# One more SwiGLU pair by seven products, neighbouring tiles paired, and the last weights' sums moved

## The chip, the cores and the metric

The kernel runs on one core of one Trainium2 chip, in one launch. The metric is the device time of that launch in microseconds (us), the median of the runs; less is better. The engines are named as in the profile: PE is TensorE's matmul, PEld its weight load, DVE is VectorE, ACT is ScalarE, POOL is GpSimd, SP is SyncE, which here issues all DMAs (SPq is its queue).

## What is computed

One decoder block on 512 tokens of width 1024, everything in float32. The reference, cut to what matters:

```python
def reference(x, norm1_g, w_in, b_in, conv_..., lru_..., w_mix_out, norm2_g, ffn_w1, ffn_w3, ffn_w2, norm_f_g):
    h = rmsnorm(x, norm1_g)
    z = h @ w_in + b_in                                   # 512x1024 @ 1024x6656
    z_glu, z_rx, z_rg, z_ga, z_gb = split(z)
    u = z_glu[:, :1024] * sigmoid(z_glu[:, 1024:])
    u = silu(layernorm(causal_depthwise_conv(u, 31 taps)))
    y_a = u @ conv_w_out + conv_b_out                     # 1024x1024
    hb = rg_lru(causal_depthwise_conv(z_rx, 4 taps))      # gated linear recurrence
    y_b = (hb * gelu(z_rg)) @ lru_w_out                   # 1280x1024
    m = sigmoid(z_ga) * y_a + sigmoid(z_gb) * y_b
    x = x + m @ w_mix_out                                 # "mixing", 1024x1024
    h = rmsnorm(x, norm2_g)
    x = x + (silu(h @ ffn_w1) * (h @ ffn_w3)) @ ffn_w2    # 1024x2816 twice, 2816x1024
    return rmsnorm(x, norm_f_g)
```

## The kernel before

**Matmuls in three parts.** Every float32 operand is split into a high part (ScalarE casts it, L127) and a low part (VectorE or GpSimd subtracts, L123), and each product is made of three matmuls, high by high, high by low and low by high (`mm3`, L489). Activations lie as 128 channels by 512 tokens. A weight chunk is a 128 x 1024 tile of 512 KB: SP loads it into one of 4 `raw` buffers (L152, or L265, L334 and L337 for chunks of several loads), ScalarE casts it, and VectorE or GpSimd subtracts, into one of 5 `hl` buffers. Chunks are worked off in one written list; `weights(key)` asks for a chunk and has those up to 4 further on emitted too (`AHEAD`).

**Seven products instead of eight.** Some matrix products are made by a Winograd form of Strassen's scheme: both operands are cut into 2 x 2 quarters, seven products of quarters stand for eight, and sums of quarters are made beside. For the SwiGLU layer (the two products with `ffn_w1` and `ffn_w3`, 22 column tiles of 128, in 11 pairs) the pairs in `SEVEN` go that way: `ffn_seven(k)` makes seven products (L1131) of 24 matmuls each for each of the two matrices' halves, 168 in all with 256 columns, where a plain pair has 96 with 512. The sums of weight quarters (t1 to t4) of these pairs are made early by GpSimd in pieces (`make_f_sums`: two loads of 256 KB, L357; four subtractions or additions, L123 and L364; a store of the sums to DRAM, L368), a piece every few steps of the input products, and are loaded again as chunks when the pair's turn comes.

**Mixing and the last product** (`ffn_w2`) go through the class `Sevenfold` (matmuls at L938). A finished pair of tiles waits in `waiting` until `release` calls `pair`, which makes the operand's sums on VectorE: one 512-wide low part and five 256-wide steps. `run` then goes over the pairs twice: first three products a pair, then the others. The second loop's operands (`late`) are split by ScalarE and VectorE, two splits a pair. The weight sums of the last product are made in 22 pieces on VectorE during the SwiGLU pairs (`out_step`, numbers per pair in `OUT_PIECES`). `KEPT` says how many finished pairs stay waiting at which pair.

**The end of mixing** (`mix_end`) is an order written by hand for TensorE, ScalarE and VectorE: the last mixing products; six adds of their banks into the rows `x` (L888); mean squares and a root (L511, L512); scaling of the rows (L1020); transposes `th` (L529) that make the SwiGLU input from the first half of the rows, while TensorE does the rest; later the same for the second half (`xs`, then `th` again). GpSimd then adds the two parts of the transposed input (`hf`, L1105) for the quarter sums `hs`.

**Order elsewhere.** A list scheduler with its own costs orders each engine's instructions, and `issue_after` ties some of them behind a named instruction. Each engine and SP's queue run their instructions strictly in that order; a DMA that has to wait for a buffer or for data holds all DMAs behind it.

The functions that the change touches, with what calls them:

Of the kernel before, what the change touches and what calls it, by code (L numbers as in the profile page):

```python
# [8 lines left out]
F32 = mybir.dt.float32  # L9
# [81 lines left out]
def tile_block(ctx, tc, a, out):  # L91
# [154 lines left out]
    class Quartered:  # L246
        def __init__(self, name, w, kh, lo, parts=()):

            self.name, self.w, self.kh = name, w, kh
            self.parts = {n: [None] * kh for n in parts}  # L250
# [5 lines left out]
            def quarter(n, k):  # L256
                if n[0] == "t":
                    return self.sums[n, k]
                i, h = int(n[1]) - 1, int(n[2]) - 1
                return w[:, k + kh * i, h * T : (h + 1) * T]  # L260
# [19 lines left out]
        def order(self):  # L280
            return [j for k in range(self.kh) for j in (k, k + self.kh)]
# [17 lines left out]
        def make_sums(self, k):  # L299
            q = [raws.tile([P, 1024], F32, tag="raw", name=f"{self.name}ws{k}_{i}") for i in range(2)]  # L300
            for i, v in enumerate(q):
                nc.sync.dma_start(v, self.w[:, k + self.kh * i, :])
# [21 lines left out]
    f_sums = {k: dram.tile([P, 4, 1024], F32, tag=f"fs{k}", name=f"fs{k}") for k in SEVEN}  # L324

    def f_quarter(n, k, w_, c0, c1):

        c, j = 4 * (int(n[1]) - 1), k + KF * (int(n[2]) - 1)
        return w_[:, c + c0 : c + c1, j * P : (j + 1) * P]

    def f_chunk(n, k):
        def load(raw_t):
            if n[0] == "t":
                newest["any"] = nc.sync.dma_start(raw_t, f_sums[k][:, IN_PLACE.index(n), :]).ins  # L334
            else:
                for i, w_ in enumerate((w1, w3)):
                    newest["any"] = nc.sync.dma_start(raw_t[:, i * T : (i + 1) * T].rearrange("p (k n) -> p k n", k=4), f_quarter(n, k, w_, 0, 4)).ins  # L337

        wchunk(f"f{n}_{k}", load, 8, P, lo=vec)

    def f_piece(k, i, c):
        four = (w1, w3)[i].rearrange("p (h k) (e n) -> p h k e n", h=2, e=2)
        at = T * i + P * c
        halves = [four[:, h, c : c + 2, :, k * P : (k + 1) * P].rearrange("p k e n -> p e k n") for h in range(2)]
        return f"{k}_{i}_{c}", halves, f_sums[k][:, :, at : at + 256]

    def o_piece(k, c):
        four = outq.w.rearrange("p (h k) (e n) -> p h k e n", h=2, e=2)
        cs = slice(256 * c, 256 * c + 256)
        return f"o{k}_{c}", [four[:, h, k, :, cs] for h in range(2)], outq.all_sums[k][:, :, cs]  # L350

    def piece_load(name, halves):
        raw = wsums.tile([P, 1024], F32, tag="wsum", name=f"fws{name}")
        for h, src in enumerate(halves):
            to = raw[:, h * T : h * T + T]
            to = to.rearrange("p (e k n) -> p e k n", e=2, k=2) if len(src.shape) == 4 else to.rearrange("p (e n) -> p e n", e=2)
            nc.sync.dma_start(to, src)  # L357
        return raw

    def piece_sums(raw, eng):  # L360
        q11, q12, q21, q22 = (raw[:, 256 * m : 256 * m + 256] for m in range(4))
# [5 lines left out]
    def piece_store(raw, dest):  # L367
        nc.sync.dma_start(dest, raw.rearrange("p (m n) -> p m n", m=4))  # L368

    def make_f_sums():  # L370
# [9 lines left out]
        while todo or sums_due or stores_due:  # L380
# [4 lines left out]
            if todo and n >= next_at:  # L385
# [5 lines left out]
                def sums(raw=raw, dest=dest):  # L391
                    with tc.issue_after(newest["sub"]):
                        piece_sums(raw, pool_e)
# [11 lines left out]
    for k in range(KF):  # L405
        if k in SEVEN:
            for n in ("b11", "b21", "b22", "t2", "t1", "t3", "t4"):
                f_chunk(n, k)
        else:
            for j in (k, k + KF):  # L410
# [487 lines left out]
    class Sevenfold:  # L898
        def __init__(self, q):
# [3 lines left out]
        def tile(self, j, make):  # L903

            k, i = j % self.kh, j // self.kh
# [4 lines left out]
            if i:  # L910
                self.waiting.append((k, *self.uv[k]))
                self.release()
# [27 lines left out]
        def run(self, sums, begun, end):  # L940
# [7 lines left out]
            late = []  # L948
            r1, r2 = ([bank(f"{n}{r}{i}") for i in range(2)] for r in ("r1", "r2"))
            r5 = [bank2(f"{n}r5{i}") for i in range(2)]  # L950
            for k in range(kh):
# [10 lines left out]
                late.append((split(f"{n}eb{k}", e, vec), split(f"{n}vb{k}", va, vec)))  # L962
# [48 lines left out]

    def mix_end(second, plus, r1, r2, r7, third):
        sc = [[longt(f"xs{t}{h}") for h in range(2)] for t in range(NT)]
# [10 lines left out]
        with tc.manual_schedule(engines={ET.PE, ET.Activation, ET.DVE}):  # L1024
# [23 lines left out]
            for t in (2, 3):  # L1048
                scaled(t, 0)

# [3 lines left out]
    o7 = Sevenfold(outq)  # L1054
    out_todo = [o_piece(k, c) for k in range(OUT_EARLY, KF) for c in range(2)]
    out_at, out_quota = [None, None], dict(OUT_PIECES)

    def out_step(k):
# [5 lines left out]
        if out_at[0]:  # L1064
            with tc.issue_after(newest["now"]):
                piece_sums(out_at[0][0], vec)
# [16 lines left out]
    first_two = [0, KF]  # L1083
# [37 lines left out]

    def ffn_seven(k):
        u_, v_ = longt(f"ou{k}"), longt(f"ov{k}")

        def product(ps, x_, w_, again=False):

            h, l = weights(f"f{w_}_{k}")
            for i in range(2):
                for c, (xh, xl) in enumerate(f_in[x_]):
                    for m, (lw, rx_) in enumerate(((h, xh), (h, xl), (l, xh))):  # L1130
                        pe.matmul(  # L1131
                            ps[:, HALVES[i]], lw[:, 4 * i + c, :], rx_, start=not (again or i or c or m),
                            stop=bool(i and c == 3 and m == 2), skip_group_check=True,
                        )

# [36 lines left out]
    for k in range(1, KF):  # L1172
# [4 lines left out]
        for j in (k, k + KF):  # L1177
# [6 lines left out]
    assert not out_todo  # L1184
# [6 lines left out]
    def loads(k):  # L1191

        if k < 2:
            out_step(None)
        elif k < 10:
            assert out_at == [None, None]
            t, h = divmod(k - 2, 2)
            nc.sync.dma_start(x2[t][h], x2_kept[t][h][:, :])
        else:
# [86 lines left out]
```

## Time and profile before

| | us |
|---|---|
| median of 3 runs | 804.78 (804.7, 804.78, 807.82) |
| profiled execution, whole | 805.14 |
| its span | 803.2 |
| input products and what runs beside them | 11 to 328 |
| products of the two mixers | 328 to 419 |
| mixing, second norm | 419 to 476 |
| first tiles by plain products (pairs 0 and 1) | 459 to 507 |
| seven SwiGLU pairs by seven products | 507 to 648 |
| two plain pairs (9 and 10) | 648 to 691 |
| last product and last norm | 691 to 803 |

The profile is one execution on the chip. Its page gives busy time and instruction count of each engine, and the chain of work that ended last, followed back from the end. Queries of the trace give the waits of an engine, its instructions in order of time (start, duration, engine, line, operation, output and inputs, count, and in brackets the idle time before and what ended it), and busy time by stretches (the length, then for each engine its busy time and in brackets its instructions, then the granted clock, the DMA engines' busy share and GB/s). A busy engine that is not on the chain sets no time by itself.

### The profile page before, as it was taken

Reading aid. Unit: us, or ns where it says so; the run is one execution under the profiler, and the core shown is the slowest. Engines: PE = TensorE matmul, PEld = TensorE weight load, DVE = VectorE, ACT = ScalarE, POOL = GpSimd, SP = SyncE. Lnnn points to the kernel's source line nnn. Section 1 sums busy time; section 2 is a strip of 40 time slices with the busy share of each in tenths; the row PEclk is TensorE's granted clock in tenths of the full one; section 3 lists DMA queues with packets and bytes.
Section 4 is the critical chain, followed back from the end, with each engine's and each line's share of the span. In section 5 each row is a group of like instructions: output and inputs, shape, how many; then the busy total and the mean of one; then the engine's idle time right before and its main releaser. Section 6 shows DMA issues by size and latency. Waiting matters only on the chain.

```text
span 803.2 us, 12106 instructions
## 1 busy us (share of the span) xinstructions
PE 792.8 (99%) x4254; PEld 687.7 (86%) x4254; DVE 676.3 (84%) x1080; ACT 457.8 (57%) x650; POOL 252.3 (31%) x203
## 2 busy tenths in 40 slices
PE   8999999999999999999999999999999999999996
PEld 7988888888888888888888898999999988888885
DVE  5799999998999998886798869979977796898556
ACT  7446788766589655653336454446555543476443
POOL 2576678756677684231320043000000000000000
PEclk9999999999999999999999999999999999999999
DMA  7746575666657743679988427699887979698552
GB/s 221 189 122 179 155 206 166 188 189 200 188 170 233 213 144 102 196 230 277 291 278 259 152 92 233 193 305 290 290 263 237 266 243 300 196 316 288 176 166 104
DMA packets 213871, 170.79 MB, mean 213 GB/s; under 512 B 13383, under 2 KB 188915, under 8 KB 213811
## 3 DMA queue, kind: packets, MB, share of 16 engines
q1 hardware_dynamic: 213811, 170.03, 69.6%
q8 instruction: 33, 0.54, 0.3%
q14 instruction: 27, 0.22, 0.1%
HBM read 134.47 MB, written 32.51 MB: 208 GB/s over the span
## 4 chain that ended last, share of the span: by engine, by line
PE 98%; DVE 1%; DMA 1%; ACT 0%; issue 0%; SPq 0%
PE z L489 35%; PE fr L1131 18%; PE or L938 13%; PE f L489 11%; PE yb L489 7%; PE ya L489 5%; PE mxr L938 5%; PE g L810 3%; DMA x<-in_x_dram 1%; PE z L582 0%; PE th L529 0%; PE tx L540 0%; DVE of L1209 0%; DVE x2b L888 0%; ACT n1j L511 0%
## 5 line engine op out<-in xcount | busy, mean ns | idle before, releaser
L683 DVE SCALAR_TENSOR_TENSOR cv<-u,par,cv 128x511 f32<-128x511 f32 (+17 forms) x240 | 162.6, 728 | 1.1 <-ACT cv L680 0.9
L123 POOL TENSOR_TENSOR hl_in<-raw_in,hl_in 128x1024 fp32r<-128x1024 f32 x51 | 123.1, 2417 | 82.6 <-ACT hl_in L127 61.1
L123 POOL TENSOR_TENSOR fws<-fws 128x256 f32<-128x256 f32 x84 | 70.8, 844 | 79.7 <-DMA fws<-in_ffn_w_dram 65.3
L127 ACT CAST hl_in<-raw_in 128x1024 fp32r<-128x1024 f32 x51 | 53.0, 1042 | 1.2 <-issue 1.0
L127 ACT CAST hl_ob<-raw_ob 128x1024 fp32r<-128x1024 f32 (+1 forms) x23 | 23.4, 1016 | 37.1 <-PE f L489 16.1
L1131 PE MATMUL fr<-hs_0h,hl_ft 128*128 128x256 f32 x224 | 41.5, 283 | 0.0
L489 PE MATMUL z<-h10h,hl_in 128*128 128x512 f32 (+1 forms) x110 | 41.4, 378 | 0.0
L123 DVE TENSOR_TENSOR hl_ft<-raw_ft,hl_ft 128x1024 fp32r<-128x1024 f32 x28 | 34.0, 1219 | 8.7 <-ACT hl_ft L127 8.7
L489 PE MATMUL z<-h11h,hl_in 128*128 128x512 f32 (+1 forms) x110 | 41.1, 376 | 0.0
L489 PE MATMUL z<-h17h,hl_in 128*128 128x512 f32 (+1 forms) x110 | 41.1, 376 | 0.0
L489 PE MATMUL z<-h13h,hl_in 128*128 128x512 f32 (+1 forms) x110 | 41.1, 376 | 0.0
L489 PE MATMUL z<-h14h,hl_in 128*128 128x512 f32 (+1 forms) x110 | 41.1, 376 | 0.0
L489 PE MATMUL z<-h15h,hl_in 128*128 128x512 f32 (+1 forms) x110 | 41.1, 376 | 0.0
L489 PE MATMUL z<-h16h,hl_in 128*128 128x512 f32 (+1 forms) x110 | 41.1, 376 | 0.0
L489 PE MATMUL z<-h12h,hl_in 128*128 128x512 f32 (+1 forms) x110 | 41.1, 376 | 0.0
L123 DVE TENSOR_TENSOR hl_ob<-raw_ob,hl_ob 128x1024 fp32r<-128x1024 f32 (+1 forms) x23 | 27.1, 1177 | 15.8 <-ACT hl_ob L127 15.5
L127 ACT CAST hl_ft<-raw_ft 128x1024 fp32r<-128x1024 f32 x28 | 29.3, 1048 | 15.4 <-issue 5.2
L123 DVE TENSOR_TENSOR hl_fb<-raw_fb,hl_fb 128x1024 fp32r<-128x1024 f32 x21 | 26.7, 1273 | 13.1 <-ACT hl_fb L127 13.1
L1131 PEld LDWEIGHTS fr<-hs_0h,hl_ft 128*128 128x128 f32 x224 | 35.4, 192 | 0.0
L127 ACT CAST hl_fb<-raw_fb 128x1024 fp32r<-128x1024 f32 x21 | 22.0, 1049 | 22.9 <-DMA raw_fb<-in_ffn_w_dram 9.7
L1131 PE MATMUL fr<-hs_0l,hl_ft 128*128 128x256 f32 x112 | 31.7, 283 | 0.0
L123 DVE TENSOR_TENSOR hl_ot<-raw_ot,hl_ot 128x1024 fp32r<-128x1024 f32 (+1 forms) x17 | 20.0, 1191 | 11.5 <-ACT hl_ot L127 11.2
(938 smaller groups left out, 2608.0 us busy)
## 6 DMA issues: line engine op xcount, KB each, us to landing
raw_in<-in_w_in_dram SPq DMA_DIRECT2D x52, 512.0 KB
fws<-in_ffn_w_dram SPq DMA_DIRECT2D x56, 256.0 KB
fs<-fws SPq DMA_DIRECT2D x28, 512.0 KB
raw_ft<-fs SPq DMA_DIRECT2D x28, 512.0 KB
fwso<-in_ffn_w_dram SPq DMA_DIRECT2D x44, 256.0 KB
ot<-fwso SPq DMA_DIRECT2D x22, 512.0 KB
raw_fb<-in_ffn_w_dram SPq DMA_DIRECT2D x42, 256.0 KB
raw_ob<-in_ffn_w_dram SPq DMA_DIRECT2D x33, 256.0 KB
```

The lines of the kernel that those rows point to most:

```text
L123: return eng.tensor_tensor(out=o, in0=x, in1=y, op=ALU.subtract)
L127: copy(h, full)
L489: pe.matmul(ps, l, r, start=i == 0, stop=i == n - 1)
L683: vec.scalar_tensor_tensor(out=acc[c][:, s:], in0=u[c][:, : T - s], scalar=dw(c, s), in1=acc[c][:, s:], op0=ALU.mult, op1=ALU.add)
L810: pe.matmul(ps, l, r, start=k == 0, stop=k == len(mms) - 1)
L938: pe.matmul(banks[i], l_[:, ts], r_, start=start and n == 0, stop=stop and n == 2, skip_group_check=again)
L1131: pe.matmul(ps[:, HALVES[i]], lw[:, 4 * i + c, :], rx_, start=not (again or i or c or m), stop=bool(i and c == 3 and m == 2), skip_group_c ...
```

## The change

- Pair 9 of the SwiGLU layer goes by seven products too: eight pairs do, three are plain (0, 1 and 10).
- Pair k is made of the neighbouring tiles 2k and 2k + 1 instead of k and k + 11. The second quarter row of weights is loaded for both tiles in one chunk (256 columns in a run), one chunk for each of `ffn_w1` and `ffn_w3`, and so are the sums; a chunk then serves two products, and the first product's chunk stays as it was.
- The 16 further instructions of sums on GpSimd come with a denser plan (from step 34 on every second step, before from step 55).
- Three of the 22 pieces of the last weights' sums are made by GpSimd inside `mix_end`; the other 19 stay on VectorE, spread differently.
- More finished pairs stay waiting (`KEPT`, up to 6), and the last stage's first loop releases one of them per step. Its late splits start at its sixth step instead of its first.

```diff
-OUT_PIECES = {1: 4, 2: 2, 3: 1, 4: 2, 5: 1, 6: 1, 7: 1, 8: 2, 9: 4, 10: 4}
-SEVEN = (2, 3, 4, 5, 6, 7, 8)
+OUT_PIECES = {1: 4, 2: 2, 3: 1, 4: 2, 5: 2, 6: 1, 7: 2, 8: 1, 9: 2, 10: 2}
+SEVEN = (2, 3, 4, 5, 6, 7, 8, 9)
-SUMS_DENSE = 55
-KEPT = {5: 1, 6: 2, 7: 3, 8: 4, 9: 2}
+SUMS_DENSE = 34
+OUT_MIX, LATE_LAG = 3, 5
+KEPT = {4: 1, 5: 2, 6: 3, 7: 4, 8: 5, 9: 6, 10: 6}
...
-        wchunk(f"f{n}_{k}", load, 8, P, lo=vec)
+        wchunk(f"fb11_{k}", load, 8, P, lo=vec)
+        for n in ("b2", "t0", "t1"):
+            for i, w_ in enumerate((w1, w3)):
+                if n == "b2":
+                    src = w_[:, 4:8, 2 * k * P : 2 * (k + 1) * P]
+                else:
+                    src = f_sums[k][:, i, int(n[1]), :].rearrange("p (k n) -> p k n", k=4)
+                wchunk(f"f{n}{i}_{k}", src, 4, 2 * P, lo=vec)
...
-outq = Quartered("o", a["ffn_w2"][0].rearrange("(k p) n -> p k n", p=P), NF // 2, vec)
+outq = Quartered("o", a["ffn_w2"][0].rearrange("(k p) n -> p k n", p=P), NF // 2, vec, step=2)
...
 # Sevenfold.run, first loop
-                late.append((split(f"{n}eb{k}", e, vec), split(f"{n}vb{k}", va, vec)))
+                if k >= self.lag:
+                    split_late()
                 begun(k)
 # second loop
                 second(k, *get(k, "b22", "t2", "t3"))
+                split_late()
...
     def mix_end(second, plus, r1, r2, r7, third):
+        made = []
+        for _ in range(OUT_MIX):
+            name, halves, dest = out_todo.pop(0)
+            with tc.issue_after(newest["any"]):
+                made.append((piece_load(name, halves), dest))
+            piece_sums(*made[-1], pool_e)
...
+        for m in made:
+            with tc.issue_after(newest["any"]):
+                piece_store(*m)
...
-    o7 = Sevenfold(outq)
+    o7 = Sevenfold(outq, LATE_LAG)
...
 # ffn_seven: product
-            h, l = weights(f"f{w_}_{k}")
+            n, e, first = WHERE[w_]
             for i in range(2):
+                if n == "b11":
+                    if i == 0:
+                        got["b11"] = weights(f"fb11_{k}")
+                    h, l = (v[:, 4 * i : 4 * i + 4, :] for v in got["b11"])
+                else:
+                    if first:
+                        got[n, i] = weights(f"f{n}{i}_{k}", AHEAD - i)
+                    h, l = (v[:, :, e * P : (e + 1) * P] for v in got[n, i])
...
+                if i == 0 and n != "b11" and not first:
+                    emit_to(emitted[0] + 1)
...
 # last stage's first loop
     def loads(k):
-        if k < 2:
-            out_step(None)
+        o7.release(max(len(o7.waiting) - 1, 0))
+        out_step(("or", k))
```

More of the change, by code (lines that the diff above doesn't have):

```diff
@@ L280, in order @@
         def order(self):
-            return [j for k in range(self.kh) for j in (k, k + self.kh)]
+            return [self.tile(k, i) for k in range(self.kh) for i in range(2)]
         def get(self, k, *names, ahead=AHEAD):
@@ L898, in tile_block, with __init__ @@
     class Sevenfold:
-        def __init__(self, q):
+        def __init__(self, q, lag=0):
+            self.lag, self.kept = lag, 0
             self.q, self.uv, self.ops, self.waiting = q, [], [], []
@@ L911, in tile @@
                 self.waiting.append((k, *self.uv[k]))
-                self.release()
+                self.release(self.kept)
         def release(self, keep=0):
@@ L948, in run, with split_late @@
             late = []
+            def split_late():
+                k = len(late)
+                if k < kh:
+                    late.append((split(f"{n}eb{k}", self.ops[k][2], vec), split(f"{n}vb{k}", self.ops[k][3], vec)))
             r1, r2 = ([bank(f"{n}{r}{i}") for i in range(2)] for r in ("r1", "r2"))
@@ L1010, in tile_block @@
     xs = []
+    out_todo = [o_piece(k, c) for k in range(OUT_EARLY, KF) for c in range(2)]
     def mix_end(second, plus, r1, r2, r7, third):
+        made = []
[4 more added lines that the diff above has]
+            piece_sums(*made[-1], pool_e)
         sc = [[longt(f"xs{t}{h}") for h in range(2)] for t in range(NT)]
@@ L1176, in tile_block @@
         o7.release(KEPT.get(k, 0))
-        for j in (k, k + KF):
+        o7.kept = KEPT.get(k, 0)
+        for j in (2 * k, 2 * k + 1):
             p1, p3 = bank(f"f1_{j}"), bank(f"f3_{j}")
```

72 lines of the change are left out of this document (37 added, 35 removed).

## The prediction

> **What bounds the kernel now.** I read the page first (engine shares, the chain that ended last), then the waits of the matmul engine, then windows by stage, then the timelines of VectorE, ScalarE, GpSimd and the DMA queue around mixing.
>
> ```profile
> span 803.2 us, 12106 instructions
> PE 792.8 (99%) x4254; PEld 687.7 (86%) x4254; DVE 676.3 (84%) x1080; ACT 457.8 (57%) x650; POOL 252.3 (31%) x203
> PE 98%; DVE 1%; DMA 1%; ACT 0%; issue 0%; SPq 0%
> ```
>
> The third line is the chain's share by engine. TensorE works 792.8 of 803.2 us; what is left is the start, 7 us of tail and about a microsecond of waits. Nothing shortens this kernel by more than the matmul time it removes plus those ends. The chain in order of time prices the two ways of doing a SwiGLU pair (columns: start, us, what):
>
> ```profile
> 506.57 141.11 PE fr L1131 x1176
> 647.68 43.55 PE f L489 x192
> ```
>
> L1131 holds the seven-product matmuls (256 columns), L489 here the plain ones (512 columns). Seven pairs are 1176 = 7 x 168 matmuls: 141.11 / 7 = 20.16 us a pair, 0.120 us each. Two plain pairs are 192: 43.55 / 2 = 21.78 us a pair, 0.227 us each. Windows over one seven-product pair, the last plain pair and the first part of the last stage (columns: length, then busy us of PE, PEld, DVE, ACT, POOL, then clock, DMA share, GB/s):
>
> ```profile
> 546.90:567.10 20.20, 20.20 (x170) 20.20 (x170) 18.91 (x32) 12.70 (x20) 0.00 (x0) 1.00 0.95 300
> 627.60:647.70 20.10, 20.10 (x169) 20.10 (x168) 14.32 (x21) 10.37 (x14) 0.00 (x0) 1.00 0.93 277
> 669.50:691.20 21.70, 21.70 (x97) 17.96 (x96) 12.45 (x27) 6.01 (x8) 0.00 (x0) 1.00 0.78 251
> 691.20:725.00 33.80, 33.80 (x151) 27.99 (x150) 32.51 (x55) 23.19 (x33) 0.00 (x0) 1.00 0.85 275
> ```
>
> TensorE is full in each at clock 1.00; VectorE is full only where the last stage begins.
>
> **Part 1, one more pair by seven products (pair 9).** It removes 96 plain matmuls and adds 168 short ones: 20.16 - 21.78 = -1.62 us, all on the path. On VectorE it adds three weight splits of 1.22 us and five adds of 0.68 us, 7.1 us, in a pair where it was busy 21.17 of 21.8 us already (from 647.7). Much of that was sums of waiting pairs, which part 4 moves; what remains is a normal seven-product pair, 14.32 us in 20.1. Cost nothing; if that cover failed it would be a few us.
>
> The Trainium skill ("TensorE: Matmul & The Clock Gate", Back-to-back issue gap) gives N/2.4 + 2.5 ns for an isolated matmul: by estimate 109 ns at 256 columns and 216 ns at 512, so 18.3 against 20.7 us, a saving of 2.4 us instead of 1.62 and 803.2 us in the end. The trace differs: 0.120 and 0.227 us, with the weight loads busy for all of each seven-product window, and its rows decide.
>
> **Part 2, neighbouring tiles paired, weights of two tiles loaded together.** Pair k is now tiles 2k and 2k+1. Two thirds of the unsummed seven-product weights come in runs of 256 columns instead of 128, with the same bytes. The DMA share was 0.87 to 0.98 in the first four such pairs and no matmul waited, so this can only help what already costs nothing. The price is a buffer held over two products: of five split buffers, the shortest lead is from the middle of a pair's third product to the middle of its sixth, three products of 24 x 0.120 = 2.88 us: 8.64 us instead of the former four, 11.5. Cast (1.05) and split (1.22) with the longest waits in these pairs (4.2 for a load, 2.3 for the cast) make 8.8 in the worst case, which rarely falls together. Taken at nothing, at most 0.2 us a pair, 1.6 in all.
>
> **Part 3, GpSimd's share.** First, four more pieces of summed weights for pair 9, taken more densely from step 34 on. That is 16 instructions at 0.844 us, 13.5 us, beside the input products. Between 205 and 305 us GpSimd is busy some 73 of 100 us. Its low-part splits (2.4 us) could now queue behind one or two pieces (3.1 us each), against four chunks of 5.44 us in hand: nothing. The last piece is loaded about one product step (5.44 us) later, so the DMA queue's wait for its sums, which ended at 412.3, ends near 418; the mixing weight behind it is needed by TensorE at 435: nothing.
>
> Second, three pieces of the last weights' sums run on GpSimd in the end of mixing: 12 instructions at 0.74 to 0.84 us, 9 to 10 us. GpSimd stood idle there for 60 us, but its neighbour does not. Timeline rows of VectorE (start, us, ..., idle before in brackets), the last two of them beside GpSimd's L1105 adds:
>
> ```profile
> 447.41 1.22 DVE L123 TENSOR_TENSOR hl_f<-raw_f,hl_f 128x1024 fp32r<-128x1024 f32 x1 [1.43 <-ACT hl_f L127]
> 448.56 4.07 DVE L888 TENSOR_TENSOR x<-mxr,x 128x512 f32<-128x512 f32 x6
> 453.72 0.89 DVE L1020 TENSOR_SCALAR xs<-x,stats 128x512 f32<-128x512 f32 x2
> 476.90 4.03 DVE L123 TENSOR_TENSOR hl_f<-raw_f,hl_f 128x1024 fp32r<-128x1024 f32 x2
> 486.77 2.31 DVE L123 TENSOR_TENSOR hl_fb<-raw_fb,hl_fb 128x1024 fp32r<-128x1024 f32 x1
> ```
>
> A 1024-wide split takes 1.22 us alone and 2.0 (4.03 / 2) to 2.31 us beside GpSimd. The split at 447.41 runs straight into the six adds, these into two squares and roots, these into the scaling at 453.72, and TensorE begins the transposes that read the scaled rows at 454.45, with about 0.2 us to spare. The three loads are queued behind one weight load that was issued at 438.96; six issues of 0.63 us and some 3 to 4 us to land put GpSimd's sums at about 444 to 455. So this split grows by 4.03/2 - 1.22 = 0.8 us; the 0.2 to spare set against one stretched scaling, TensorE waits 0.8. Bounds: nothing, if the sums fall elsewhere or the slack holds; 1.7 us if three of the scalings (0.44 us each) are stretched in the same ratio, 0.29 each. Adds that read PSUM beside GpSimd kept their time (0.74 at 407.38), so I take 0.8, the row nearest in kind.
>
> The Trainium skill ("GPSIMD Engine Reference", Specifications) says that GpSimd shares its SBUF interfaces with VectorE and that contention arises with instructions that have two SBUF inputs or run in a two-port mode. The splits agree (2.0 against 1.22); no row here shows a scaling beside GpSimd, and by the page it would be stretched too, which by estimate would make the wait 1.7 us rather than 0.8.
>
> The stores of these sums stand on SP's queue ahead of the loads of pair 1's weights, which were issued from 440 to 450 before and now go at about 456. ScalarE casts the first of them near 462; landing near 460 it is in time. This is a rival below.
>
> **Part 4, sums of waiting pairs beside the last stage.** A pair's sums are a 512-wide split and five 256-wide steps; by the distance of their starts in the timeline, 0.60 + 5 x 0.335 = 2.3 us. Before, one pair's (the last) fell in the last stage; now six are released there, one per step, though the changed order starts several before the stage begins, in the 21.70 - 12.45 = 9.3 us that VectorE idles in the last plain pair. That is up to 5 x 2.3 = 11.4 us more at the stage's start; against it 5 x 2 late splits (0.60 each, 6.0 us) go to the second half of the stage, and two fewer pieces of weight sums (8 x 0.335 = 2.7 us) reach it. Net 2.7 us, and the idle time ahead of the stage covers it: nothing. Without that cover it is 2.7 us at most.
>
> **Sum.** -1.62 + 0.8 = -0.8 us. The profiled execution took 805.14 (span 803.2 and 1.94 around it), 0.36 over the median of 804.78. So 804.3 on its scale, **804.0 us** on that of the median.
>
> **Rivals.**
>
> - *Clean gain*: the mixing sums miss the split. For it: loads may land late. Against: the transposes start on the heels of the scaling. 804.78 - 1.62 = 803.2.
> - *Slower, through SP's queue*: the piece at 347.56 shows GpSimd taking 4.49 us for two instructions, 2.25 each, beside VectorE. Twelve at that rate take 27 us, to 471. The store then holds SP until then, pair 1's weights land at 475, and ScalarE's in-order queue has their cast ahead of the squares for the second half of the rows, whose transposes were due at 470.5. Cast, square, root, scale (some 4 us) follow: transposes at 479, 8.5 us late: 804.8 - 1.6 + 8.5 = 811.7. It decides once the twelve average over about 1.55 us (sums to 463, weights at 467.5, rows at 471). Against: 0.74 to 0.84 in nearly all pieces, and VectorE's work there mostly reads PSUM.
> - *VectorE becomes the bound where the last stage begins*: released sums stand ahead of weight splits on its queue, TensorE waits for weights. Full price 2.7 us on top of the forecast: 806.7. Against: pairs are ready four to five steps of 4.08 us ahead.
> - *Weight lead too short in the seven-product pairs*: 8 x 0.2 = 1.6 us, 805.6.
> - *The change doesn't do what it says*: more is saved because some wait goes that I don't see. TensorE's waits sum to 3.2 us, 2.7 of them at the start, which stays; so hardly below 801.
>
> **How the numbers follow.** About 0.5% (4 us) is what a measurement of this kernel can tell from no change. Chances: forecast 0.60, clean gain 0.17, short lead 0.07, VectorE 0.06, SP's queue 0.08, unseen gain 0.02. The likeliest is 804.0 with its own range 803.1 (no wait) to 804.9 (1.7 us wait). The range takes in the clean gain less 0.6 for run-to-run spread, 802.6, and the short lead and nearly the whole VectorE case, 806.6; SP's queue stays out. Faster by over 0.5% (below 800.8): 0.02. Slower (above 808.8): SP's queue, 0.08. Same: 0.90.
>
> **What would show it.** In the changed profile: 4326 matmuls; 1344 at the seven-product line in 161.3 us; GpSimd rows on the last weights at about 444 to 455; the split ahead of the six adds at 2.0 us instead of 1.22; a gap of 0.5 to 1 us on TensorE ahead of the first transposes and no other new one. A gap ahead of the second transposes, or at the first products of the last stage, would make the prediction wrong; so would a seven-product pair over 20.3 us.

## The result, and the profile after

The changed kernel took 804.29 us (median of 22 runs, 803.82 to 805.72) against 805.5 us for the kernel before in the same runs (22 runs, 804.67 to 807.97). The medians lie 1.21 us apart. The ratio is 0.9982, 95% interval 0.9976 to 0.9988 (it leaves disturbed runs out), which on 805.5 us is 1.45 us less, 1.0 to 1.9. The forecast was 804.0 us and 0.8 us less. The profiled execution took 804.0 us with a span of 802.2, 1.0 us under the span before.

From the page of the changed kernel, its size, the work of each engine and the shares of the chain of waits:

```profile
span 802.2 us, 12279 instructions
PE 791.7 (99%) x4326; PEld 690.6 (86%) x4326; DVE 680.1 (85%) x1076; ACT 463.0 (58%) x658; POOL 273.9 (34%) x231
PE 96%; DVE 1%; DMA 1%; ACT 0%; issue 0%; SPq 0%; DVEq 0%
```

There are the 72 more matmuls (168 - 96), and 28 more instructions on GpSimd (16 and 12). The third line is the chain: TensorE's share fell from 98% to 96%. The chain in order of time (start, us, what) shows where it left TensorE. Before:

```profile
419.09 35.36 PE mxr L938 x156
454.45 0.87 PE th L529 x8
```

After:

```profile
418.72 27.21 PE mxr L951 x120
...
448.97 1.90 DVE x L900 x3
...
452.36 1.64 DVE xs L1049 x2
...
454.10 0.77 DVE xs L1049
454.92 0.98 PE th L541 x7
...
507.13 161.27 PE fr L1177 x1344
668.40 21.79 PE f L501 x96
690.19 102.97 PE or L951 x453
```

(L951 was L938, L541 was L529, L1049 was L1020, L1177 was L1131, L501 was L489, L900 was L888, L126 was L123.) Before, the mixing products ran unbroken for 35.36 us into the transposes. Now the chain leaves TensorE for the adds and scalings of VectorE, and the transposes (all but the first) wait for the third scaling. TensorE's waits (us in total, times, longest) have it as the only one that was not there before:

```profile
PE th L541 <- DVE xs L1049: 0.7, 1, 0.7
```

Further down the chain stand eight seven-product pairs in 161.27 us and one plain pair in 21.79.

The two spans compared piece by piece (starts of the chain's rows, us):

| from - to | before | after | difference |
|---|---|---|---|
| start to mixing | 419.09 | 418.72 | -0.37 |
| mixing to the first seven-product pair | 87.48 | 88.41 | +0.93 |
| pairs 2 to 10 | 184.66 | 183.06 | -1.60 |
| last stage and end | 111.97 | 112.01 | +0.04 |
| span | 803.2 | 802.2 | -1.00 |

The first row is chance (the kernel before, profiled once more below). So the profiles place -1.60 + 0.93 + 0.04 = -0.63 us; the interval of the ratio begins at -1.0. The 0.4 us or more between them has no place in any trace here.

VectorE and GpSimd where the transposes wait (timeline rows: start, us, engine, line, operation, what, in brackets the idle time ahead):

```profile
447.04 1.22 DVE L126 TENSOR_TENSOR hl_f<-raw_f,hl_f 128x1024 fp32r<-128x1024 f32 x1 [1.43 <-ACT hl_f L130]
...
452.36 1.64 DVE L1049 TENSOR_SCALAR xs<-x,stats 128x512 f32<-128x512 f32 x2
...
454.10 1.62 DVE L1049 TENSOR_SCALAR xs<-x,stats 128x512 f32<-128x512 f32 x2
```

```profile
447.05 1.81 POOL L377 TENSOR_TENSOR fwso<-fwso 128x256 f32<-128x256 f32 x1
...
451.28 0.74 POOL L377 TENSOR_TENSOR fwso<-fwso 128x256 f32<-128x256 f32 x1
452.10 2.48 POOL L126 TENSOR_TENSOR fwso<-fwso 128x256 f32<-128x256 f32 x3
```

The split began 0.01 us ahead of a GpSimd instruction. It kept its 1.22 us, and the GpSimd instruction took 1.81 instead of 0.74. The scalings came into a row of GpSimd instructions, and two of them took 1.64 us instead of 0.89. In both meetings the one that began first kept its time. The Trainium skill ("SBUF — State Buffer", Who interferes with whom) calls this an exclusive lock on a pair of ports that the two engines share; of VectorE's two-port modes it says that whoever issues first holds the pair for the whole instruction while the other waits. These rows agree, and the split, which has two inputs, behaves the same way; a run below with 32 more instructions on GpSimd does not agree.

### The profile page after: what moved, and what is told of

The parts are those of the page before. It is cut to its first block, busy times and chain, and to the rows that moved or that the text cites. A ratio compares the mean times of both kernels' runs of the same rounds, so it can differ in the third digit from the quotient of the medians.

```text
span 802.2 us, 12279 instructions
## 1 busy us (share of the span) xinstructions
PE 791.7 (99%) x4326; PEld 690.6 (86%) x4326; DVE 680.1 (85%) x1076; ACT 463.0 (58%) x658; POOL 273.9 (34%) x231
## 4 chain that ended last, share of the span: by engine, by line
PE 96%; DVE 1%; DMA 1%; ACT 0%; issue 0%; SPq 0%; DVEq 0%
PE z L501 35%; PE fr L1177 20%; PE or L951 13%; PE f L501 8%; PE yb L501 7%; PE ya L501 5%; PE mxr L951 4%; PE g L822 3%; DMA x<-in_x_dram 1%; DVE x L900 0%; PE th L541 0%; PE z L594 0%; PE tx L552 0%; DVE xs L1049 0%; DVE of L1257 0%
## 5 line engine op out<-in xcount | busy, mean ns | idle before, releaser
L126 POOL TENSOR_TENSOR hl_in<-raw_in,hl_in 128x1024 fp32r<-128x1024 f32 x51 | 123.2, 2419 | 68.8 <-ACT hl_in L130 55.7
L126 POOL TENSOR_TENSOR fws<-fws 128x256 f32<-128x256 f32 x96 | 79.0, 825 | 83.7 <-DMA fws<-in_ffn_w_dram 79.4
L1177 PE MATMUL fr<-hs_0h,hl_ft 128*128 128x256 f32 x256 | 47.4, 283 | 0.0
L126 DVE TENSOR_TENSOR hl_fb<-raw_fb,hl_fb 128x1024 fp32r<-128x1024 f32 x24 | 30.4, 1267 | 18.8 <-ACT hl_fb L130 18.8
L126 DVE TENSOR_TENSOR hl_ft<-raw_ft,hl_ft 128x1024 fp32r<-128x1024 f32 x32 | 38.9, 1219 | 7.3 <-ACT hl_ft L130 7.3
L501 PE MATMUL z<-h10h,hl_in 128*128 128x512 f32 (+1 forms) x110 | 41.4, 378 | 0.0
L501 PE MATMUL z<-h17h,hl_in 128*128 128x512 f32 (+1 forms) x110 | 41.1, 376 | 0.0
L501 PE MATMUL z<-h11h,hl_in 128*128 128x512 f32 (+1 forms) x110 | 41.1, 376 | 0.0
L501 PE MATMUL z<-h16h,hl_in 128*128 128x512 f32 (+1 forms) x110 | 41.1, 376 | 0.0
L501 PE MATMUL z<-h14h,hl_in 128*128 128x512 f32 (+1 forms) x110 | 41.1, 376 | 0.0
L501 PE MATMUL z<-h13h,hl_in 128*128 128x512 f32 (+1 forms) x110 | 41.1, 376 | 0.0
L501 PE MATMUL z<-h15h,hl_in 128*128 128x512 f32 (+1 forms) x110 | 41.1, 376 | 0.0
L501 PE MATMUL z<-h12h,hl_in 128*128 128x512 f32 (+1 forms) x110 | 41.1, 375 | 0.0
L1177 PEld LDWEIGHTS fr<-hs_0h,hl_ft 128*128 128x128 f32 x256 | 40.5, 192 | 0.0
L130 ACT CAST hl_ft<-raw_ft 128x1024 fp32r<-128x1024 f32 x32 | 33.2, 1044 | 9.1 <-DMA raw_ft<-fs 2.9
L130 ACT CAST hl_fb<-raw_fb 128x1024 fp32r<-128x1024 f32 x24 | 25.2, 1050 | 21.3 <-DMA raw_fb<-in_ffn_w_dram 11.4
L1177 PE MATMUL fr<-hs_0l,hl_ft 128*128 128x256 f32 x128 | 36.2, 283 | 0.0
L126 DVE TENSOR_TENSOR hl_ob<-raw_ob,hl_ob 128x1024 fp32r<-128x1024 f32 (+1 forms) x23 | 26.9, 1175 | 10.5 <-ACT hl_ob L130 10.5
L1185 ACT ACTIVATE c<-c 128x256 f32<-128x256 f32 x24 | 10.1, 419 | 32.4 <-DVE c L900 32.4
```

What stands on the lines that cost most here:

```text
L126: return eng.tensor_tensor(out=o, in0=x, in1=y, op=ALU.subtract)
L130: copy(h, full)
L501: pe.matmul(ps, l, r, start=i == 0, stop=i == n - 1)
L1177: pe.matmul(ps[:, HALVES[i]], lw[:, c, :], rx_, start=not (again or i or c or m), stop=bool(i and c == 3 and m == 2), skip_group_check=True,)
L1185: act.activation(c[:, LO], c[:, LO], AF.Silu)
```

## The experiments

"Ratio" is always against the kernel before; unless said, an edit is made in the changed kernel.

**The last weights' sums back on VectorE.**

```diff
-OUT_MIX, LATE_LAG = 3, 5
-OUT_PIECES = {1: 4, 2: 2, 3: 1, 4: 2, 5: 2, 6: 1, 7: 2, 8: 1, 9: 2, 10: 2}
+OUT_MIX, LATE_LAG = 0, 5
+OUT_PIECES = {1: 4, 2: 2, 3: 2, 4: 2, 5: 2, 6: 2, 7: 2, 8: 2, 9: 2, 10: 2}
```

> The changed kernel with all 22 pieces of the last weights' sums on VectorE, none on GpSimd at the end of mixing. Theory (GpSimd's instructions hold up the scaling of the rows, and this is the only cost of the change): the 0.72 us gap ahead of the first transposes is gone, the two scalings take 0.89 us a pair again instead of 1.64, and the time is 0.7 us under the changed kernel, ratio to before about 0.9973 instead of 0.9982. Rival (VectorE has no room for three more pieces, 12 instructions of 0.42 us): the gap goes, but a new one of up to 5 us comes in the SwiGLU pairs or at the start of the last stage.

Measured: 804.09 us, ratio 0.9981 [0.9972, 0.999]. From its VectorE timeline:

```profile
452.00 0.89 DVE L1049 TENSOR_SCALAR xs<-x,stats 128x512 f32<-128x512 f32 x2
452.99 0.88 DVE L1049 TENSOR_SCALAR xs<-x,stats 128x512 f32<-128x512 f32 x2
```

Without GpSimd beside them the scalings take 0.89 us again, the wait at the transposes is gone, and mixing to the first seven-product pair is 87.46 us, as before the change (87.48). So the 0.93 us of that row come from the three pieces on GpSimd. VectorE made them during the pairs without a new wait: 183.16 us from pair 2 to the last stage (after: 183.06). The ratio does not resolve the 0.95 us between the two kernels; the profiled span, 801.6, is 0.6 us shorter. Chance is of that size here: mixing began 0.36 us earlier in this profile, and what follows the start of the last stage took 0.61 us longer (112.62 against 112.01).

**The order of the scalings changed**: the halves that the first transposes read are scaled first for both row tiles, the other two behind.

```diff
-            for t in range(2):
-                scaled(t, 1)
+            r_0 = rstd_end(begun[0], x2[0][1], sc[0][1])
+            scale(0, 0, r_0)
+            r_1 = rstd_end(begun[1], x2[1][1], sc[1][1])
+            scale(1, 0, r_1)
+            scale(0, 1, r_0)
+            scale(1, 1, r_1)
```

> The changed kernel with the four scalings in another order: the halves that the first transposes read go first. If a GpSimd instruction in flight holds a scaling off until it ends (a lock): two scalings instead of three stand before the first transposes, each waits for at most one GpSimd instruction (0.74 us), gap 0.2 us or none. If the two engines share bandwidth and all scalings are stretched by the same factor: xs of the second row tile is ready 0.4 to 0.8 us earlier all the same, so the gap goes as well; the durations tell the two apart: one of four scalings at 0.5 us and others near 1.2 for the lock, all near 0.8 for sharing.

Measured: 803.91 us, ratio 0.9979 [0.9971, 0.9988]. TensorE has no wait on `xs` in the list of waits. Its VectorE timeline:

```profile
452.11 0.76 DVE L1047 TENSOR_SCALAR xs<-x,stats 128x512 f32<-128x512 f32 x1
452.98 2.52 DVE L1047 TENSOR_SCALAR xs<-x,stats 128x512 f32<-128x512 f32 x3
```

The scalings are held as long as ever (3.28 us for four; 1.64 + 1.62 in the changed kernel), but the first transposes need only the first two. The other two are late for the second group, whose eight transposes stretch from 0.87 to 1.37 us. Mixing to the first pair takes 88.08 us, between 87.46 and 88.41: the wait is divided, and 0.62 of the 0.95 us stays. One by one the four scalings took 0.76, 0.77, 0.95 and 0.96 us. This is not the pattern that was expected of a lock (one at 0.5, others near 1.2); by durations alone it looks more like shared bandwidth. The ends of the instructions decide it, under the next run.

**Each GpSimd sum in two halves of 128 columns**: 24 instructions instead of 12, the same work.

```diff
-            piece_sums(*made[-1], pool_e)
+            for w in range(2):
+                raw_, of_ = made[-1][0], slice(128 * w, 128 * w + 128)
+                q11, q12, q21, q22 = (raw_[:, 256 * m : 256 * m + 256][:, of_] for m in range(4))
+                ...
```

> The changed kernel with the 12 GpSimd instructions at the end of mixing cut in two, 24 of 128 columns. Lock theory: a scaling waits for at most one of them, about half as long as before; the gap of 0.72 us falls to 0.2 to 0.4 us. Sharing theory: the same bytes in the same time, the gap stays at 0.7 us or grows with the longer sums.

Measured: 804.84 us, ratio 0.998 [0.996, 1.0]; this execution began mixing 1.7 us late for a wait at its start. Its VectorE timeline:

```profile
454.07 1.31 DVE L1055 TENSOR_SCALAR xs<-x,stats 128x512 f32<-128x512 f32 x2
455.49 1.09 DVE L1055 TENSOR_SCALAR xs<-x,stats 128x512 f32<-128x512 f32 x2
```

From the start of mixing to the transposes behind the gap it is 35.61 us, against 36.20 in the changed kernel and 35.36 before. GpSimd works a little longer (2.56 us for six halves of the second piece; 2.26 for three wholes), but a scaling waits for at most half as long an instruction: 1.31 instead of 1.64, then 1.09 instead of 1.62. The price follows the length of one GpSimd instruction, not the amount of work beside, which speaks for a lock and against a share of bandwidth. Where the instructions end says the same (single rows of the timelines; us):

| kernel | VectorE's instruction | took | ended | GpSimd's ended | between |
|---|---|---|---|---|---|
| changed | first scaling | 0.76 | 453.12 | 452.84 | 0.28 |
| changed | second scaling | 0.96 | 454.00 | 453.72 | 0.28 |
| halves | first scaling | 0.71 | 454.78 | 454.50 | 0.28 |
| halves | fourth scaling | 0.67 | 456.57 | 456.29 | 0.28 |
| before | split at 476.90 | 1.79 | 478.69 | 477.61 | 1.08 |

However long a scaling took, it ended 0.28 us after a GpSimd instruction had ended (0.28 or 0.29 for all twelve of these two kernels and of the one with the other order). Two engines that share bandwidth would have no such fixed distance; an engine that is let in when the other ends has.

**The same sums about 26 us earlier**, loads and all ahead of the loads of the rows `x2`.

```diff
+    made = []
+    for _ in range(OUT_MIX):
+        name, halves, dest = out_todo.pop(0)
+        made.append((piece_load(name, halves), dest))
+        piece_sums(*made[-1], pool_e)
     x2 = [[longt(f"x2{t}{h}") ...
```

> The changed kernel with the loads and GpSimd sums of the three pieces put ahead of the load of the rows, so that they run at about 418 to 430 us beside the first loop of mixing; stores where they were. Theory: VectorE's splits there are held up by up to 0.74 us each but have microseconds to spare; no gap ahead of the first transposes, time 0.7 us under the changed kernel, ratio to before 0.9973. Rival (the mixing weights' splits are late): a new gap of 0.5 to 2 us between 420 and 450 us, ratio 0.998 or more.

Measured: 807.09 us, ratio 1.0019 [1.0005, 1.0033]. From its waits of TensorE, its SP queue and its ScalarE timeline:

```profile
PE mxr L951 <- DVE x L900: 2.9, 2, 1.5
```

```profile
414.37 4.02 SPq L366 DMA_DIRECT2D fwso<-in_ffn_w_dram  x6
418.43 1.07 SPq L271 DMA_DIRECT2D raw_mxb<-in_w_mix_out_dram  x2
```

```profile
424.83 1.05 ACT L130 CAST hl_mxb<-raw_mxb 128x1024 fp32r<-128x1024 f32 x1 [7.20 <-DMA raw_mxb<-in_w_mix_out_dram]
```

The scalings are back at 0.88 us. But six piece loads of 4.02 us now stand ahead of the mixing weights on SP's queue, and ScalarE waits 7.20 us for one of these (in the changed kernel the same cast ran at 418.80). TensorE then waits 2.9 us in mixing. A queue held ahead of weights does cost, where the weights are wanted at once. It is not the only cost here: the sums hold VectorE's instructions at their new place as well (three splits took 1.58 to 1.76 us instead of 1.22), and some of these stand in the chain behind the late weight. This run does not part the two.

**Seven pairs by seven products instead of eight.**

```diff
-SEVEN = (2, 3, 4, 5, 6, 7, 8, 9)
+SEVEN = (2, 3, 4, 5, 6, 7, 8)
```

> The changed kernel, but pair 9 is again made by two tiles of plain matmuls; all else of the change stays. Term 1 alone: 4254 matmuls, two plain pairs in about 43.6 us and 1176 seven-product matmuls in about 141.1 us, so the span is 1.62 us over that of the changed kernel (802.2 + 1.6 = 803.8) and the ratio to the kernel before about 1.000. Rival (the pair's saving is paid back in VectorE work or in the last stage, so removing it costs less): under 0.8 us over the changed kernel, ratio 0.999 or less. Rival (something else of the change saves time): ratio clearly below 1.

Measured: 805.62 us, ratio 1.0004 [0.9993, 1.0014]. Its chain:

```profile
507.00 141.11 PE fr L1177 x1176
648.12 43.55 PE f L501 x192
691.66 102.93 PE or L951 x453
```

Pairs 2 to 10 take 184.66 us, 1.60 more than with eight; the span is 803.7, 1.5 more. Removing the pair removes the gain, and what is left of the change is neither faster nor slower than the kernel before.

**The pairing of neighbouring tiles alone.** All of the change's numbers are set back to those before (`SEVEN`, `SUMS_DENSE`, `OUT_PIECES`, `KEPT`; `OUT_MIX` and `LATE_LAG` 0); the pairing and its loads stay, and the call that releases waiting pairs in the last stage's first loop.

> The kernel before with the pairing of neighbouring tiles alone: seven pairs by seven products, the old quotas of weight pieces and of kept pairs, no sums on GpSimd in the end of mixing, late splits all in the first half of the last stage. Theory (the pairing costs and brings nothing on the path): ratio 1.000 within 0.0007, span 803.2 within 0.5, seven-product pairs at 20.15 us each. Rival (the shorter lead of the weights makes TensorE wait): up to 0.2 us a pair, 1.4 us more, ratio 1.0017, with waits at the seven-product line. Rival (it is the pairing that brings part of the gain): ratio 0.999 or less.

Measured: 804.71 us, ratio 0.9993 [0.9984, 1.0001], span 802.8. Mixing to the first pair 87.47 us (before 87.48), pairs 184.66 (184.66): to 0.01 us the same, with seven pairs in 141.11 us in both. Nothing waits for the shorter lead.

**The late splits all in the first half of the last stage.**

```diff
-OUT_MIX, LATE_LAG = 3, 5
+OUT_MIX, LATE_LAG = 3, 0
```

> The changed kernel, but all late splits of the last stage stand in its first half, as in the kernel before. This puts five times two splits of 0.60 us, 6.0 us of VectorE work, back into the first 33.8 us of the stage, where VectorE was busy 32.7. Theory (work ahead of the stage and the distance of four to five steps cover it): at most 1 us over the changed kernel, ratio 0.998 to 0.9995. Rival (VectorE is the bound there, as the third rival of the prediction says): 32.7 + 6.0 = 38.7 us of work in 33.8, so up to 4.9 us of waits on TensorE in the first half of the last stage, ratio 1.001 to 1.004.

Measured: 804.21 us, ratio 0.9986 [0.9977, 0.9995]. Windows of the first half of the last stage, here and in the changed kernel (length, then busy us and instructions of PE, PEld, DVE, ACT, POOL, then clock, DMA share, GB/s):

```profile
690.71:724.51 33.80, 33.80 (x151) 28.00 (x150) 33.66 (x60) 23.52 (x36) 0.00 (x0) 1.00 0.58 184
```

```profile
690.19:724.00 33.81, 33.81 (x151) 28.00 (x150) 32.71 (x58) 22.36 (x34) 0.00 (x0) 1.00 0.70 219
```

VectorE is full, 33.66 of 33.80 us, and TensorE still does not wait: it is busy in all of the window in both, and the stage's chain row lasts 102.96 us (102.97). The window holds only 0.95 us more of VectorE's work, since other work slid into the second half, and nothing waited for that either. A full engine is no bound as long as what it makes is wanted later.

This profile shows one thing more, in mixing, where the edit changes nothing. VectorE and GpSimd:

```profile
446.99 1.79 DVE L126 TENSOR_TENSOR hl_f<-raw_f,hl_f 128x1024 fp32r<-128x1024 f32 x1 [1.43 <-ACT hl_f L130]
```

```profile
446.15 1.54 POOL L126 TENSOR_TENSOR fwso<-fwso 128x256 f32<-128x256 f32 x2 [30.83 <-DMA fwso<-in_ffn_w_dram]
```

The second of these two GpSimd instructions began at 446.96, 0.03 us ahead of the split. Here it is the split that waits: 1.79 us instead of 1.22. The scalings are held as before, and mixing to the first seven-product pair takes 88.98 us, 1.50 over the kernel before instead of 0.93. Which engine pays is decided by hundredths of a microsecond, and the same code in `mix_end` came out both ways.

**GpSimd busy for 13 us more.** Behind the third piece's sums, ahead of its store:

```diff
             piece_sums(*made[-1], pool_e)
+            if len(made) == OUT_MIX:
+                for i_ in range(32):
+                    q_ = made[-1][0][:, 128 * (i_ % 2) : 128 * (i_ % 2) + 128]
+                    pool_e.tensor_tensor(out=q_, in0=q_, in1=ones, op=ALU.mult)
```

> The changed kernel with 32 more GpSimd instructions behind the sums of the third piece, each of 128 columns and about 0.4 us (they multiply by ones, so the values stay), so that the last store of these sums leaves SP's queue about 13 us later, near 469 instead of 456. Rival of the prediction (stores of slow GpSimd sums hold SP's queue): pair 1's weights are issued near 469 and land near 473, so a gap of 5 to 8 us opens ahead of the second transposes or the first products of pair 1; ratio 1.005 to 1.009. Other theory (only the shared port matters, the queue has room): under 1 us more than the changed kernel, ratio below 0.9995.

Measured: 808.26 us, ratio 1.0032 [1.0016, 1.0047]: neither of the two. From its waits of TensorE and the timelines of GpSimd, SP's queue and VectorE:

```profile
PE f L501 <- DVE hl_f L126: 2.5, 1, 2.5
```

```profile
457.60 13.41 POOL L1045 TENSOR_TENSOR fwso<-fwso,ones 128x128 f32<-128x128 f32 x32
```

```profile
471.04 0.52 SPq L381 DMA_DIRECT2D ot<-fwso  x1
471.60 1.85 SPq L155 DMA_DIRECT2D raw_f<-in_ffn_w_dram  x2
```

```profile
464.42 7.67 DVE L126 TENSOR_TENSOR hl_f<-raw_f,hl_f 128x1024 fp32r<-128x1024 f32 x1 [0.79 <-ACT hl_f L130]
```

The store did hold SP's queue to 471.04, and two weight loads went out at 471.60. But TensorE did not wait for these. It waited 2.5 us for a split whose weights had come long before: it took 7.67 us instead of 1.22 and ended 1.1 us after GpSimd's last extra instruction (471.01). Mixing to the first pair is 91.84 us, 3.43 over the changed kernel. GpSimd shut VectorE out over some fifteen instructions, not for the rest of one, which is more than the lock as told above gives. It need not happen each time: of the ten runs one took 803.95 us, the time of the changed kernel, and the others 807.08 to 811.49.

**The same row of GpSimd work on another tile**, so that no store waits for it.

```diff
+            summed = piece_sums(*made[-1], pool_e)
+        for _ in range(32):
+            with tc.issue_after(summed):
+                pool_e.tensor_tensor(out=ones, in0=ones, in1=ones, op=ALU.mult)
```

> The run before this with 32 more GpSimd multiplications of 128 columns gave 3.4 us more from mixing to the first seven-product pair; a split of VectorE that began at 464.42 took 7.67 us, until GpSimd's last extra instruction ended at 471.01, and the third store left SP's queue only then. This run has the same 32 multiplications, on a tile of ones that no store reads, so the third store leaves at about 456 as in the changed kernel. Theory (GpSimd's uninterrupted row of instructions keeps VectorE's two-input split out): the split is held again until about 471, 6 to 8 us long, and the matmuls of pair 0 wait 2 to 3 us for it; 3 to 4 us over the changed kernel, ratio 1.002 to 1.004. Rival (it was the held store): under 0.5 us over the changed kernel, ratio 0.998 to 0.9995.

Measured: 804.12 us, ratio 0.9972 [0.996, 0.9984]. GpSimd and VectorE:

```profile
456.50 16.40 POOL L1044 TENSOR_TENSOR ones<-ones 128x128 f32<-128x128 f32 x32
```

```profile
463.46 1.23 DVE L126 TENSOR_TENSOR hl_f<-raw_f,hl_f 128x1024 fp32r<-128x1024 f32 x1 [0.78 <-ACT hl_f L130]
```

The theory's number was wrong: 32 GpSimd instructions around the split, and it takes 1.23 us. Taken alone this speaks for the held store. But one thing more differs: on the one tile each multiplication must wait for the one before, while in the run before two neighbours worked on different halves and could overlap. The single rows show it: on the halves an instruction starts every 0.42 us and lasts 0.47, on the one tile every 0.48 and lasts 0.40.

**A row of fills instead**, which read nothing (80 of `pool_e.memset(ones, 1.0)` in the place of the 32).

> As the run with the free tile of ones, but the extra row is 80 GpSimd fills of 128 columns, which read no tile (one such fill took 0.20 us alone at the start of the kernel, so the row lasts 10 to 16 us, to 468 to 473). Theory (only GpSimd instructions that read SBUF shut out VectorE's two-input instructions): the split takes 1.22 us, no wait on the matmuls, ratio 0.998 to 0.9995; the scalings of the second rows near 466, one input each, are the ones that may be held, up to 0.8 us. Rival (any GpSimd instruction shuts it out): a split of 5 us or more and a ratio of 1.001 or more.

Measured: 807.54 us, ratio 1.0018 [1.0008, 1.0029]. GpSimd, VectorE and TensorE's new wait:

```profile
457.41 21.70 POOL L1044 MEMSET ones<- 128x128 f32 x80
```

```profile
463.57 1.23 DVE L126 TENSOR_TENSOR hl_f<-raw_f,hl_f 128x1024 fp32r<-128x1024 f32 x1 [0.78 <-ACT hl_f L130]
```

```profile
PE fr L1180 <- DVE hl_ft L126: 1.3, 1, 1.3
```

The split is not held, but the fills also stood in turn (one of 0.20 us every 0.26), so this does not tell reading from pausing. The row lasted longer than planned, to 479.1, and so GpSimd's adds of the transposed input (`hf`) began at 479.08 instead of 472.38. VectorE's work behind them came late, and the seven-product pairs waited 1.3 us. So the run leaves its question open, and shows what 7 us more on GpSimd cost there.

**The kernel before once more.**

> The kernel before, unchanged, profiled a second time and timed against itself. Its first profile began mixing at 419.09 us, 0.37 later than that of the changed kernel; 0.3 of it is a wait of 0.4 us of the weight loads near 181 us for a transfer of the halo rows. If that wait and the later start are part of the kernel (every kernel with paired tiles that was profiled without a late start had begun mixing at 418.4 to 418.7), they come again, and the changed kernel gains 0.4 us there; if they are chance, mixing begins at 418.4 to 418.8. The ratio to itself should be 1.000 within 0.001.

Measured: 805.87 us, ratio 1.0001 [0.999, 1.0011]. Mixing begins at 418.62 us and no weight load waits for the halo rows: the -0.37 us in the table is chance. Its seven pairs took 141.35 us instead of 141.11, so a few tenths between two single profiles mean nothing by themselves.

**The long row on the third piece again, each instruction waiting for the one before.** Against the first of these runs:

```diff
-                    q_ = made[-1][0][:, 128 * (i_ % 2) : 128 * (i_ % 2) + 128]
+                    q_ = made[-1][0][:, :128]
```

> As the first run with 32 more GpSimd multiplications on the third piece (7.67 us for a split of VectorE, ratio 1.0032), but each multiplication now works on the same 128 columns and so waits for the one before it; in the first run two neighbours in the row were independent (0.42 us each), and on the tile of ones, where each waited for the one before (0.51 us each), no split was held. The store of the third piece is again late, near 472. Theory (VectorE gets in only where GpSimd pauses between two instructions): the split near 463 takes 1.2 to 1.9 us, no wait of 2 us or more on the matmuls of pair 0, ratio 0.997 to 0.9995; and as the store is late without a held split, this is the test of the queue: if loads behind a store that leaves near 472 still come in time, no gap opens ahead of the second transposes or pair 1. Rival 1 (two different tiles as inputs, not the missing pause, hold the split): split of 5 us or more again, ratio 1.002 to 1.004. Rival 2 (the held store counts): no held split, but a gap ahead of pair 1 of 1 us or more, ratio above 1.000.

Measured: 804.24 us, ratio 0.9983 [0.9973, 0.9993], span 802.2. GpSimd, VectorE and SP's queue:

```profile
456.41 18.52 POOL L1045 TENSOR_TENSOR fwso<-fwso,ones 128x128 f32<-128x128 f32 x32
```

```profile
463.23 1.23 DVE L126 TENSOR_TENSOR hl_f<-raw_f,hl_f 128x1024 fp32r<-128x1024 f32 x1 [0.78 <-ACT hl_f L130]
```

```profile
474.96 0.52 SPq L381 DMA_DIRECT2D ot<-fwso  x1
475.57 1.57 SPq L1054 DMA_DIRECT2D x2k<-x  x2
477.24 0.59 SPq L155 DMA_DIRECT2D raw_f<-in_ffn_w_dram  x1
```

The inputs, their number and the work are those of the run with 7.67 us, and the store leaves even later (474.96). The split takes 1.23 us, no wait opens, and mixing, the pairs and the last stage begin at the same hundredth as in the changed kernel. So neither the two different tiles nor the held store was the cause; what was taken away is the overlap of neighbouring GpSimd instructions (one starts every 0.54 us and lasts 0.46). The instruction at 463.45 took 1.32 us instead: there GpSimd waited for the split.

But overlap alone does not shut VectorE out. In the kernel before, GpSimd's adds of the transposed input overlap too (476.32, 1.29 us long, then 477.57), and the split at 476.90 came in between these two. With the sums in halves, instructions of 128 columns also started every 0.42 us, and a split that began among them at 448.75 took 1.23. So taking the overlap away was enough here, and what more it takes for a row to shut VectorE out stays open. The queue is cleared only in part: of the three weight loads that stood behind the store in the run with 7.67 us, the scheduler put two ahead of it in this kernel.

## Why the prediction was right, and where it was not

- **Part 1 (-1.62)** was right: -1.60 between the two profiles, and 1.60 again between the runs with eight and with seven pairs. Eight pairs take 161.27 us against the 161.3 foretold, 20.16 each.
- **Part 2 (0)** was right: from mixing to the last stage the pairing alone changes nothing by more than 0.01 us.
- **Part 3, the wait (+0.8)**: the size was right (0.72 as a wait, 0.93 with the pieces around it), the place was wrong. The step that failed is "so this split grows by 4.03/2 - 1.22 = 0.8 us". I took the 2.0 us of splits that start while GpSimd works for a price of nearness. Here the split came first by 0.01 us, kept 1.22, and GpSimd paid. The price fell on the scalings, which the sum had left at nothing: 0.75 us for the first two, where the upper bound had 0.29 each. The Trainium skill's row that the prediction cites ("GPSIMD Engine Reference", Specifications) names two-port instructions beside those with two inputs; no row here shows in which mode a scaling runs, only that it was held. The wait stayed under 1.7 only because the split stayed out of the sum. Two errors of opposite sign came to the right total, and that is luck: in the profile of the run with the early late splits GpSimd was first by 0.03 us, split and scalings both paid, and the row cost 1.50 us, near the upper bound of 1.7.
- **Part 3, SP's queue (0)**: its wait for the sums of the SwiGLU weights ended at 413.6, not near 418 (before: 412.3). The term was mis-sized, and its worth is nothing either way.
- **Part 4 (0)** was right: the last stage is 0.04 us longer. VectorE's 18.07 busy us in the last plain pair (12.45 before) show the sums that were started ahead of the stage. Even the 6 us of late splits put back make no wait.
- **The rivals**: clean gain fell by the 0.72 us wait. VectorE's bound and the short lead fell by the runs made for them. SP's queue did not occur: the twelve sums ended at 456.3, averaging 0.94 us. With the store at 471 and 475 instead of 456, beyond its condition, it never gave its 8.5 us; in the second of these kernels only one load still stood behind the store. What came there, a split shut out for 6.4 us, was on no list of mine.
- **The total**: 0.8 us forecast, 0.63 us placed by the traces, 1.45 [1.0, 1.9] by the clock. The fastest of the 22 runs of each kernel lie 0.85 us apart (804.67 and 803.82). What the difference is stays open. The run with the pieces back on VectorE saves 0.95 us in the trace and 0.0001 in the ratio, so ratios of these kernels do not settle half a microsecond.

## What to carry to other kernels

Before work is given to an idle engine, look at which instructions of its neighbour it will meet, and in which order they start: the price is mostly the rest of one instruction, paid by whoever comes second. Where the starts lie within a few hundredths of a microsecond, reckon with both orders. If the second stands on the critical path, cut the work into shorter instructions or let the critical ones go first. And if a long GpSimd row shuts VectorE out, let each of its instructions depend on the one before: in the one case tried here that was enough.

## What the runs showed of the hardware

- A scaling with one tile as input, 512 columns, is held by GpSimd just as a subtraction with two is: two took 0.89 us alone, 1.64 beside 256-column sums, 1.31 and 1.09 beside 128-column ones, and 1.09 beside the row of 32 that stood in turn.
- Both engines can be the one that is held: GpSimd's 0.74 us became 1.81 where the split had begun 0.01 us ahead, and the split's 1.22 became 1.79 where GpSimd had begun 0.03 us ahead.
- A held scaling ended 0.28 or 0.29 us after a GpSimd instruction, whatever time it took; a held split 1.08 us after it (478.69 after 477.61, 472.09 after 471.01).
- One row of 32 GpSimd instructions that overlap shut a split out for its whole rest (7.67 us instead of 1.22); the same row in turn did not (1.23). Other overlapping rows did not either. VectorE's instructions on PSUM ran through both rows at their usual 0.48 us.
